# A two-layer decoder trunk on one core: weight products in runs of 16 hi parts and 16 lo parts

## The chip, the core and the metric

The kernel runs on one core of a Trainium2 chip. The metric is the device time of one execution in microseconds, the median of three runs. The engines that matter are TensorE (PE in the profile, with its weight loads shown apart as PEld), VectorE (DVE), ScalarE (ACT) and the queue of SyncE (SP), which issues the transfers of the weights.

## The reference

Two layers work on 256 tokens of 2048 features in float32. Each layer is a token mixer, a SwiGLU feed-forward block of 5632 hidden features and a gated per-layer embedding, each with an RMS norm ahead of it, and a final norm ends the trunk. The mixer of layer 0 is a Mamba-2 state-space mixer (an input projection to 10,304 columns, a convolution, a chunked scan, an output projection from 4096), that of layer 1 an RG-LRU (an input projection to 4096 columns, a convolution, block-diagonal gates, a scan, an output projection). Nearly all arithmetic is products of activations with weight matrices:

```python
h = h + mixer(rms_norm(h, norm_mix[i]))
v = rms_norm(h, norm_ffn[i])
gate, up = jnp.split(v @ w_ffn_in[i], 2, axis=-1)
h = h + (jax.nn.silu(gate) * up) @ w_ffn_out[i]
h = h + jax.nn.sigmoid(rms_norm(h, norm_ple[i]) @ w_ple_gate[i]) * (p[i] @ w_ple_up[i])
```

(The last lines are put in short form; the reference does the same in its own functions.)

## The kernel before

Activations lie with features on the 128 partitions and tokens on the free axis. A float32 operand of a product is held as two float32r parts, hi and lo, that add up to it. An activation operand x is one tile of 128 x 512: its hi part in the first 256 columns, its lo part in the last. A product of one weight block of 128 x 128 with one operand is two matmuls (`mm`, line 238): the weight's hi part times all 512 columns, which fills one bank of 512 columns, and the weight's lo part times the first 256, which is added to the bank's second half. They are called the hi product and the lo product here, and both together a pair. When all contraction tiles are done, `total` (line 147) adds the two halves of the bank: a copy on ScalarE (line 151) and an addition on VectorE (line 154).

Weights come as loads of 512 KB, as a rule two contraction tiles of 512 columns. `weights` (line 222) issues the transfer into one of five raw buffers, casts it to hi on ScalarE (line 234), subtracts to get lo on VectorE (line 235), with four hi tiles and four lo tiles of 1024 columns in rotation, and hands out both parts for two contraction tiles at a time.

`panel` (line 243) computes 512 output columns, as four blocks in four banks of the eight. For each contraction tile it runs four pairs, block by block, and then one step of other work (`shadow`): one of the queue `post`, which must follow the previous panel, and some of the queue `side`. The last two pairs of contraction tiles (`held=2`) are kept back and run block by block, so that the four banks finish one after another; in the very last panel of the kernel three are (`held=3`, line 676). `panel` is called by `ssd_mixer`, `lru_mixer`, `out_product`, `ffn`, `ple_up` and `ple`. The gates of the RG-LRU (line 548) call `mm` themselves.

The lines of the program are not the order of execution. The instructions of each engine are put in order when the kernel is built, by priority and by when their operands are expected, so two lines written hi, lo can stand apart on TensorE. Each engine then works strictly in its own order, and waits by semaphores for the others. At the end of the kernel, the last panel's four blocks go through sigmoid, product, addition to the residual (line 309), square and scaling, then come the last norm's root and the output.

Of the kernel before, what the change touches and what calls it, by code (L numbers as in the profile page):

```python
# [17 lines left out]
P = 128  # L18
T = 256                 # tokens
D = 2048  # L20
KT = D // P             # feature tiles of the residual
FFN = 5632
EPS = 1e-6
PW = 512                # output columns of one panel
NB = PW // P            # output tiles of one panel
KG = 2                  # contraction tiles of one weight load

# columns of the packed per-channel vectors
# [13 lines left out]
class Trunk:  # L42
    """Activations lie feature-major (feature on the partition, token on the free axis).

    A float32 operand of a product is held as two float32r parts, hi + lo, that add up to it
    exactly; a product is hi*hi + hi*lo + lo*hi in float32 accumulation.  An activation operand is
    one [128, 512] tile (hi | lo), so that the stationary weight's hi part streams both at once.
    """

    def __init__(self, ctx, tc):  # L50
        self.tc, self.nc = tc, tc.nc
        nc = self.nc
        pool = lambda name, bufs, **kw: ctx.enter_context(tc.tile_pool(name=name, bufs=bufs, **kw))
        self.const = pool("const", 1)
        self.act = pool("act", 48)
        self.wraw = pool("wraw", 5)
        self.wsp = pool("wsp", 4)
        self.tmp = pool("tmp", 2)
        self.ssd = pool("ssd", 2)
        self.ps = pool("ps", 8, space=bass.MemoryType.PSUM)  # L60
        self.side = deque()     # work in the shadow of the products, in small steps
        self.credit = 0.0
        self.last_table = None
        self.post = deque()     # what must follow a panel within the next one, in small steps

        c = self.const
        self.ident = c.tile([P, P], F32, name="ident")
        make_identity(nc, self.ident)
        self.identr = c.tile([P, P], F32R, name="identr")
        nc.vector.tensor_copy(self.identr, self.ident)  # L70
        self.sel = c.tile([P, 64], F32R, name="sel")
        nc.vector.tensor_tensor(self.sel, self.ident[:, :64], self.ident[:, 64:], ALU.add)
        self.ones = c.tile([P, P], F32, name="ones")
        nc.vector.memset(self.ones, 1.0)
        warm = c.tile([P, 1], F32, name="warm")
        nc.scalar.activation(warm, self.ones[:, :1], AF.Identity)
        # over (s, l) of one chunk, twice: s > l is put at -1e30
        mask = self.act.tile([P, 256], F32, name="mask", tag="a")
        nc.gpsimd.memset(mask, 0.0)
        for o in (0, P):  # L80
            nc.gpsimd.affine_select(
                out=mask[:, o:o + P], in_=mask[:, o:o + P],
                compare_op=ALU.is_ge, fill=-1e30, base=0, pattern=[[1, P]], channel_multiplier=-1)
        self.mask = c.tile([P, 256], F32R, name="maskr")
        nc.vector.tensor_copy(self.mask, mask)
        self.vecs = c.tile([P, NVEC], F32, name="vecs")
        self.h = c.tile([P, KT, T], F32, name="h")

# [6 lines left out]
    def table(self, out, in_, func, **kw):  # L95
        """An activation that needs its table: these keep program order, so that tables change seldom."""
# [34 lines left out]
    def split(self, src):  # L131
        """(hi | lo) operand of a [128, 256] float32 tile."""
        nc = self.nc
        x = self.act.tile([P, 2 * T], F32R, name="x", tag="a")
        nc.scalar.copy(x[:, :T], src)  # L135
        nc.vector.tensor_tensor(x[:, T:], src, x[:, :T].bitcast(F32), ALU.subtract)  # L136
        return x

    def split_scaled(self, src, w):
        """(hi | lo) operand of src * w, w one value per partition."""  # L140
# [6 lines left out]
    def total(self, b, t=None):  # L147
        """Sum of the two halves of a finished bank, in SBUF."""
# [24 lines left out]
    def rstd(self, acc, n, out, wait=4, last=False):  # L173
        """Appends to out 1 / sqrt(sum over partitions and tiles of acc / n + eps) per token, on
        every partition; in steps."""
# [12 lines left out]
        # a first guess, then Newton steps: on VectorE alone, or from the root's table where time is short  # L188
# [32 lines left out]

    def weights(self, w, width=PW, kt=KG, also=None):
        """Load w [128, kt, width]; gives its (hi, lo) parts for a few contraction tiles at a time."""
# [14 lines left out]
    def mm(self, b, hi, lo, x, first, last):  # L238
        nc = self.nc
        nc.tensor.matmul(b, hi, x, start=first, stop=False, skip_group_check=True)  # L240
        nc.tensor.matmul(b[:, T:], lo, x[:, :T], start=False, stop=last, skip_group_check=True)  # L241

    def panel(self, w, xs, pump=1.4, kt=KG, nb=NB, pre=None, post=True, held=2):
        """w [kg, 128, kt, nb*128] times the operands xs; returns the banks of the nb tiles.

        The last `held` weight tiles run block by block, so that the banks finish one after another.
        """
        banks = [self.bank() for _ in range(nb)]
        nk = w.shape[0] * kt
        k = 0  # L250
        rest = []

        def step(j, k, part):
            hi, lo = part
            self.mm(banks[j], hi[:, j * P:(j + 1) * P], lo[:, j * P:(j + 1) * P], xs[k], k == 0, k == nk - 1)

        def shadow():
            if post:
                self.advance(self.post)
            self.pump(pump)  # L260

        for g in range(w.shape[0]):
            for parts in self.weights(w[g], nb * P, kt, pre and (lambda: pre(g))):
                if k + len(rest) + held * len(parts) >= nk:
                    rest.extend(parts)
                    continue
                for i, part in enumerate(parts):
                    for j in range(nb):
                        step(j, k + i, part)
                    shadow()  # L270
                k += len(parts)
        for j in range(nb):
            for i, part in enumerate(rest):
                step(j, k + i, part)
            for _ in range((j + 1) * len(rest) // nb - j * len(rest) // nb):
                shadow()
# [5 lines left out]

    def norm_block(self, i, norm, layer, square=True):
        """Start the norm of residual block i: its square sum and its operand (without rstd)."""
# [16 lines left out]
    def norm_end(self, last=False):  # L301
        """The rstd of the norm, in steps: self.r."""
# [8 lines left out]
    def out_product(self, w, xs, norm, layer, pump=1.25, between=None, panels=range(D // PW)):  # L311
        """h += w^T xs; each finished block goes into the next norm (if there is one)."""
# [9 lines left out]

    def conv(self, t, cw, cb, ntap, i, out):
        """Causal depthwise convolution of t [128, 256] with its bias."""
# [6 lines left out]
    def softplus(self, v, n):  # L331
        """max(v, 0) + log1p(exp(-|v|)), the logarithm from its atanh series."""
# [17 lines left out]
    def ssd_mixer(self, w_dt, w_in, w_out, load):  # L350
# [3 lines left out]
        bc = [self.act.tile([P, 2, T], F32, name=f"bc{i}", tag="a") for i in range(8)]  # B, then C  # L354
# [20 lines left out]
        def dt_part(t):  # L375
# [11 lines left out]
            # columns: sums over chunk 0 | sums over chunk 1 | the latter from the start of chunk 0  # L387
# [4 lines left out]
            # the heads' hi parts on the lower partitions, their lo parts on the upper ones  # L392
# [15 lines left out]
        def of0(t):  # L408
            """The columns of a (s, l) tile whose s is in chunk 0."""
            return t[:, :384].rearrange("p (a b) -> p a b", a=3)[:, 0:3:2, :]  # L410

        def group(g, ts):
# [5 lines left out]
            # C B^T over (s, l) of the chunk pairs (0,0) (1,1) (0,1)  # L418
# [76 lines left out]
        # panels: C, dt (its 64 heads twice, on both halves of the partitions), B, x, z  # L495
# [18 lines left out]
    def lru_mixer(self, w_in, w_gates, w_out):  # L514
# [21 lines left out]
        def gates(q):  # L536
            """Blocks 2q and 2q+1 of the recurrence: channels 512 q .. 512 q + 511."""
# [3 lines left out]
            for m, (bias, dst) in enumerate((("lru_ba", rt), ("lru_bx", it))):  # L541
                ws = [t for ts in self.weights(w_gates[q, m], T, 4) for t in ts]
                for blk in range(2):
                    for j in range(2):
                        b = self.bank()
                        for k in range(2):
                            hi, lo = ws[blk * 2 + k]
                            self.mm(b, hi[:, j * P:(j + 1) * P], lo[:, j * P:(j + 1) * P],
                                    xop[q * 4 + blk * 2 + k], k == 0, k == 1)
# [21 lines left out]
            for j in range(4):  # L571
                self.table(th[j], th[j], AF.Sqrt, scale=2.0 ** 60)     # its table is poor near 0
# [50 lines left out]
    def ffn(self, layer, w_in, w_out, between):  # L623
# [18 lines left out]
        for g0, g1 in ((0, 6), (6, 11)):        # hidden panels that one pass of w_out takes  # L642
# [15 lines left out]
    def ple(self, w_gate, up, norm, nlayer):  # L658
# [15 lines left out]
        for n in range(D // PW):  # L674
            last = norm == "norm_final" and n == D // PW - 1
            ts = self.totals(self.panel(w_gate[n], u, held=3 if last else 2))
# [5 lines left out]
def trunk(ctx, tc, xT, pT, vecs, w_dt, w_ssd_in, w_ssd_out, w_lru_in, w_lru_gates, w_lru_out,  # L682
# [4 lines left out]
    def load(g):  # L687
        """The residual's blocks 2 g and 2 g + 1 and their operands."""
# [40 lines left out]

def _tiles(w, kg=KG, pw=PW):  # L730
    """[K, N] to [N / pw, K / (128 kg), 128, kg, pw]."""
# [4 lines left out]
def _cols(v):  # L736
    """[..., 128 n] to [128, ... n]."""
# [3 lines left out]
def _layout(a):  # L741
# [21 lines left out]
    g = np.stack([a["lru_wa"][0], a["lru_wx"][0]])              # [2, 8, 256, 256]  # L763
# [26 lines left out]
```

## Time and profile before

| | us |
|---|---|
| Median of three runs (lowest, highest) | 2738.17 (2736.03, 2739.68) |
| The profiled execution: span from first to last instruction | 2736.6 |
| TensorE products busy | 2707.5 |
| TensorE weight loads busy | 2339.8 |
| VectorE busy | 1887.4 |
| ScalarE busy | 1503.1 |
| Transfers | 495.24 MB, 181 GB/s in the mean |

The page gives no time of the profiled execution but its span, so the span is compared with the runs. A product's recorded duration reaches from its start to its modelled end, and neighbours overlap: 399 ns of a hi product's record stand beside a shorter distance between starts. Busy shares of TensorE are therefore read only to see that it hardly pauses. The first product starts 7.2 us into the span.

### The profile page before, as it was taken

The numbers are of one execution on the slowest core, as the hardware profiler recorded it, in microseconds if no ns is written. First come the engines' busy times: TensorE is split into PE (matmuls) and PEld (weight loads), VectorE is DVE, ScalarE is ACT, GpSimd is POOL, SyncE is SP. The second block draws the span as 40 slices with busy tenths as digits, with TensorE's granted clock in tenths as the row PEclk, the third lists the DMA queues.
The fourth block names the chain that finished last, engine by engine and source line by source line (L and its number), as shares of the span: only waits on it lengthen the run. The fifth ranks groups of instructions, "written<-read, shape, count | busy, mean of one in ns | idle before, by whom it ended". The sixth has DMA issues, their size and how long they took to land.

```text
span 2736.6 us, 40656 instructions
## 1 busy us (share of the span) xinstructions
PE 2707.5 (99%) x15488; PEld 2339.8 (85%) x15488; DVE 1887.4 (69%) x3130; ACT 1503.1 (55%) x2397; POOL 1.4 (0%) x9
## 2 busy tenths in 40 slices
PE   8999999999999999999999999999999999999997
PEld 7888888888888888888888888888888888888886
DVE  8887878856566655566666889987666555665666
ACT  7666665544454444444455678866444444444555
POOL 0000000000000000000000000000000000000000
PEclk9999999999999999999999999999999999999999
DMA  6544455565666666656665555566666665666653
GB/s 236 184 149 140 136 155 177 178 190 179 192 183 187 185 190 186 185 185 186 191 188 181 182 170 185 171 204 191 188 186 185 187 189 179 186 187 196 189 180 122
DMA packets 136708, 495.24 MB, mean 181 GB/s; under 512 B 15296, under 2 KB 15424, under 8 KB 136512
## 3 DMA queue, kind: packets, MB, share of 16 engines
q1 hardware_dynamic: 136512, 492.65, 58.5%
q8 instruction: 121, 1.98, 0.3%
q14 instruction: 75, 0.61, 0.1%
HBM read 490.49 MB, written 2.10 MB: 180 GB/s over the span
## 4 chain that ended last, share of the span: by engine, by line
PE 95%; DVE 3%; ACT 1%; issue 0%; DMA 0%; SPq 0%; DVEq 0%; ACTq 0%
PE bank L240 61%; PE bank L241 31%; DVE lo L235 1%; PE bank L461 1%; PE bank L447 0%; PE bank L445 0%; DVE c L328 0%; DVE hs L579 0%; PE bank L463 0%; PE bank L211 0%; PE bank L431 0%; DVE c L567 0%; ACT L97 0%; DVE t L154 0%; DVE th L576 0%
## 5 line engine op out<-in xcount | busy, mean ns | idle before, releaser
L240 PE MATMUL bank<-x,hi 128*128 128x512 f32 x7440 | 2632.0, 399 | 8.8 <-DVE x L144 7.2
L241 PE MATMUL bank<-x,lo 128*128 128x256 f32 x7440 | 2079.4, 281 | 5.9 <-DVE lo L235 5.9
L240 PEld LDWEIGHTS bank<-x,hi 128*128 128x128 f32 x7440 | 1396.8, 188 | 350.8 <-DVE x L144 7.2
L235 DVE TENSOR_TENSOR lo<-raw,hi 128x1024 fp32r<-128x1024 f32 x930 | 1134.4, 1222 | 722.8 <-ACT hi L234 719.7
L234 ACT CAST hi<-raw 128x1024 fp32r<-128x1024 f32 x930 | 972.2, 1049 | 892.9 <-PE bank L240 874.0
L241 PEld LDWEIGHTS bank<-x,lo 128*128 128x128 f32 x7440 | 1403.2, 189 | 12.4 <-DVE lo L235 10.2
L151 ACT COPY s<-bank 128x256 f32<-128x256 f32 x497 | 180.9, 370 | 225.3 <-PE bank L241 224.6
L154 DVE TENSOR_TENSOR t<-bank,s 128x256 f32<-128x256 f32 x449 | 186.8, 420 | 61.4 <-ACT s L151 59.4
L161 DVE TENSOR_TENSOR t<-t,r 128x256 f32<-128x256 f32 x217 | 88.5, 419 | 1.7
L328 DVE SCALAR_TENSOR_TENSOR c<-t,vecs,c 128x255 f32<-128x255 f32 (+2 forms) x144 | 63.9, 477 | 3.4 <-ACT c L326 3.0
L309 DVE TENSOR_TENSOR h<-h,t 128x256 f32<-128x256 f32 x144 | 60.0, 421 | 2.3
L97 ACT ACTIVATE e<-bank,ncs 128x256 f32<-128x256 f32 (+1 forms) x128 | 45.6, 418 | 15.7 <-PE bank L447 9.9
L97 ACT ACT_TABLE_LOAD x41 | 52.6, 1283 | 0.9 <-DVE c L328 0.2
L143 ACT ACTIVATE x<-h,vecs 128x256 fp32r<-128x256 f32 x96 | 48.1, 509 | 7.9 <-DVE h L309 5.9
L144 DVE SCALAR_TENSOR_TENSOR x<-h,vecs,x 128x256 fp32r<-128x256 f32 x96 | 45.3, 480 | 0.3 <-ACT x L143 0.2
L452 DVE TENSOR_TENSOR e<-e,cm 128x384 f32<-128x384 f32 x64 | 35.2, 555 | 14.9 <-ACT e L97 14.2
L97 ACT ACTIVATE sg<-t 128x256 f32<-128x256 f32 x88 | 36.5, 420 | 15.9 <-DVE t L161 15.9
L135 ACT CAST x<-t 128x256 fp32r<-128x256 f32 x88 | 36.0, 409 | 16.8 <-DVE t L638 16.8
L170 ACT ACTIVATE q<-h 128x256 f32<-128x256 f32 x104 | 42.2, 408 | 4.2 <-DVE h L309 1.9
L171 DVE TENSOR_TENSOR acc<-acc,q 128x256 f32<-128x256 f32 x104 | 43.5, 418 | 0.6
L638 DVE TENSOR_TENSOR t<-t,sg 128x256 f32<-128x256 f32 x88 | 36.9, 420 | 0.7
L136 DVE TENSOR_TENSOR x<-t,x 128x256 fp32r<-128x256 f32 x88 | 36.6, 416 | 0.0
(120 smaller groups left out, 652.6 us busy)
## 6 DMA issues: line engine op xcount, KB each, us to landing
raw<-in_w_ffn_in_dram SPq DMA_DIRECT2D x352, 512.0 KB, 4.2
raw<-in_w_ffn_out_dram SPq DMA_DIRECT2D x176, 512.0 KB, 4.2
raw<-in_w_ssd_in_dram SPq DMA_DIRECT2D x160, 512.0 KB, 4.1
raw<-in_w_ssd_out_dram SPq DMA_DIRECT2D x64, 512.0 KB, 3.7
raw<-in_w_ple_gate_dram SPq DMA_DIRECT2D x64, 512.0 KB, 4.1
raw<-in_w_lru_in_dram SPq DMA_DIRECT2D x64, 512.0 KB, 4.1
raw<-in_w_lru_out_dram SPq DMA_DIRECT2D x32, 512.0 KB, 4.2
raw<-in_w_ple_up_dram SPq DMA_DIRECT2D x8, 512.0 KB, 4.4
```

The source lines that it names most:

```text
L97: i = self.nc.scalar.activation(out, in_, func, **kw).ins
L143: nc.scalar.activation(x[:, :T], src, AF.Copy, scale=w)
L144: nc.vector.scalar_tensor_tensor(x[:, T:], src, w, x[:, :T].bitcast(F32), ALU.mult, ALU.subtract)
L151: nc.scalar.copy(s, b[:, T:])
L154: nc.vector.tensor_tensor(t, b[:, :T], s, ALU.add)
L161: self.nc.vector.tensor_tensor(t, t, r, ALU.mult)
L234: nc.scalar.copy(hi, src)
L235: nc.vector.tensor_tensor(lo, src, hi.bitcast(F32), ALU.subtract)
L240: nc.tensor.matmul(b, hi, x, start=first, stop=False, skip_group_check=True)
L241: nc.tensor.matmul(b[:, T:], lo, x[:, :T], start=False, stop=last, skip_group_check=True)
L309: self.nc.vector.tensor_tensor(hb, hb, t, ALU.add)
L328: nc.vector.scalar_tensor_tensor(out[:, d:], t[:, :T - d], self.vec(cw, (3 - d) * ntap + i), out[:, d:], ALU.mult, ALU.add)
```

## The change

`mm` is gone and `panel` is rewritten. Contraction tiles are gathered until 16 products of one kind can be made (`RUN // nb`, four tiles in a panel of four blocks) or the panel's tiles end. Then the group runs: first 16 hi products, tile by tile and block by block, then 16 lo products. In a panel's last group the lo products are sorted by block. In the very last panel of the kernel (`apart`) the last group runs block by block, each with its four hi and four lo products. A step of other work is issued whenever the products so far, a hi counted as two units and a lo as one, pass another 3 x nb units. The gates' pairs are written out in place and keep their order. Comments and docstrings are taken out elsewhere, which changes nothing.

```diff
+RUN = 16
...
-    def mm(self, b, hi, lo, x, first, last):
-        nc = self.nc
-        nc.tensor.matmul(b, hi, x, start=first, stop=False, skip_group_check=True)
-        nc.tensor.matmul(b[:, T:], lo, x[:, :T], start=False, stop=last, skip_group_check=True)
...
-    def panel(self, w, xs, pump=1.4, kt=KG, nb=NB, pre=None, post=True, held=2):
+    def panel(self, w, xs, pump=1.4, kt=KG, nb=NB, pre=None, post=True, apart=False):
+        nc = self.nc
         banks = [self.bank() for _ in range(nb)]
         nk = w.shape[0] * kt
+        todo = []
+        size = RUN // nb
+        count = [0, 0]
+
+        def product(j, k, part, lo):
+            b, x, wt = banks[j], xs[k], part[lo][:, j * P:(j + 1) * P]
+            if lo:
+                nc.tensor.matmul(b[:, T:], wt, x[:, :T], start=False, stop=k == nk - 1, skip_group_check=True)
+            else:
+                nc.tensor.matmul(b, wt, x, start=k == 0, stop=False, skip_group_check=True)
+
+            count[0] += 1 if lo else 2
+            while count[0] >= 3 * nb * (count[1] + 1):
+                count[1] += 1
+                if post:
+                    self.advance(self.post)
+                self.pump(pump)
+
+        def group(last):
+            if last and apart:
+                for j in range(nb):
+                    for lo in (0, 1):
+                        for k, part in todo:
+                            product(j, k, part, lo)
+            else:
+                for k, part in todo:
+                    for j in range(nb):
+                        product(j, k, part, 0)
+                order = [(j, k, part) for k, part in todo for j in range(nb)]
+                if last:
+                    order.sort(key=lambda o: o[0])
+                for j, k, part in order:
+                    product(j, k, part, 1)
+            todo.clear()
+
         k = 0
...
         for g in range(w.shape[0]):
             for parts in self.weights(w[g], nb * P, kt, pre and (lambda: pre(g))):
...
+                for part in parts:
+                    todo.append((k, part))
+                    k += 1
+                    if len(todo) == size or k == nk:
+                        group(k == nk)
...
-            ts = self.totals(self.panel(w_gate[n], u, held=3 if last else 2))
+            ts = self.totals(self.panel(w_gate[n], u, apart=last))
```

## Rows read from the trace of the kernel before

**Rows 1.** The page: the span, and busy us, share and instructions of each engine.

```profile
span 2736.6 us, 40656 instructions
PE 2707.5 (99%) x15488; PEld 2339.8 (85%) x15488; DVE 1887.4 (69%) x3130; ACT 1503.1 (55%) x2397; POOL 1.4 (0%) x9
```

**Rows 2.** The page's groups by line: busy us, mean ns | idle before, releaser.

```profile
L240 PE MATMUL bank<-x,hi 128*128 128x512 f32 x7440 | 2632.0, 399 | 8.8 <-DVE x L144 7.2
...
L235 DVE TENSOR_TENSOR lo<-raw,hi 128x1024 fp32r<-128x1024 f32 x930 | 1134.4, 1222 | 722.8 <-ACT hi L234 719.7
L234 ACT CAST hi<-raw 128x1024 fp32r<-128x1024 f32 x930 | 972.2, 1049 | 892.9 <-PE bank L240 874.0
```

**Rows 3.** Windows, hi products alone: length, PE busy (count), PEld, granted clock, DMA.

```profile
1000.00:1380.00 380.00, 380.00 (x1076) 202.06 (x1076) 1.00 0.62 188
...
1785.00:1890.00 105.00, 105.00 (x304) 56.81 (x303) 1.00 0.62 195
```

**Rows 4.** Timeline of TensorE, two stretches in alternation: start us, duration us, what.

```profile
20.29 0.39 PE L240 MATMUL bank<-x,hi 128*128 128x512 f32 x1
...
21.33 0.40 PE L240 MATMUL bank<-x,hi 128*128 128x512 f32 x1
...
900.22 0.40 PE L240 MATMUL bank<-x,hi 128*128 128x512 f32 x1
...
901.28 0.40 PE L240 MATMUL bank<-x,hi 128*128 128x512 f32 x1
```

**Rows 5.** Timeline of TensorE where products of one kind follow each other.

```profile
71.33 1.08 PE L240 MATMUL bank<-x,hi 128*128 128x512 f32 x4
...
1623.52 1.30 PE L240 MATMUL bank<-x,hi 128*128 128x512 f32 x5
1624.65 0.28 PE L241 MATMUL bank<-x,lo 128*128 128x256 f32 x1
...
1630.61 1.09 PE L240 MATMUL bank<-x,hi 128*128 128x512 f32 x4
1631.54 0.64 PE L241 MATMUL bank<-x,lo 128*128 128x256 f32 x4
1632.01 0.39 PE L240 MATMUL bank<-x,hi 128*128 128x512 f32 x1
...
1637.91 0.87 PE L240 MATMUL bank<-x,hi 128*128 128x512 f32 x3
1638.62 0.52 PE L241 MATMUL bank<-x,lo 128*128 128x256 f32 x3
...
1686.42 1.30 PE L240 MATMUL bank<-x,hi 128*128 128x512 f32 x5
1687.56 0.64 PE L241 MATMUL bank<-x,lo 128*128 128x256 f32 x4
1688.03 0.40 PE L240 MATMUL bank<-x,hi 128*128 128x512 f32 x1
...
1746.83 0.75 PE L241 MATMUL bank<-x,lo 128*128 128x256 f32 x5
1747.42 0.40 PE L240 MATMUL bank<-x,hi 128*128 128x512 f32 x1
...
2572.30 0.76 PE L240 MATMUL bank<-x,hi 128*128 128x512 f32 x2
```

**Rows 6.** Waits: who waited for whom, us in total, times, longest us.

```profile
ACT s L151 <- PE bank L241: 224.6, 297, 4.0
...
PE bank L241 <- DVE lo L235: 5.9, 7, 1.4
```

**Rows 7.** Timeline of the end: first copy, last lo product, last block's addition.

```profile
2713.49 0.37 ACT L151 COPY s<-bank 128x256 f32<-128x256 f32 x1 [4.02 <-PE bank L241]
...
2719.53 0.28 PE L241 MATMUL bank<-x,lo 128*128 128x256 f32 x1
...
2722.37 0.42 DVE L309 TENSOR_TENSOR h<-h,t 128x256 f32<-128x256 f32 x1
```

More of the change, by code (lines that the diff above doesn't have):

```diff
@@ L249, in panel @@
         nk = w.shape[0] * kt
-        k = 0
[L251 to L260, printed above, removed]
+        todo = []
[13 more added lines that the diff above has]
+                self.pump(pump)
@@ L262, in panel @@
+        k = 0
         for g in range(w.shape[0]):
             for parts in self.weights(w[g], nb * P, kt, pre and (lambda: pre(g))):
[L264 to L276, printed above, removed]
+                for part in parts:
[3 more added lines that the diff above has]
+                        group(k == nk)
@@ L547, in gates @@
                             hi, lo = ws[blk * 2 + k]
-                            self.mm(b, hi[:, j * P:(j + 1) * P], lo[:, j * P:(j + 1) * P],
-                                    xop[q * 4 + blk * 2 + k], k == 0, k == 1)
+                            x = xop[q * 4 + blk * 2 + k]
+                            nc.tensor.matmul(b, hi[:, j * P:(j + 1) * P], x,
+                                             start=k == 0, stop=False, skip_group_check=True)
+                            nc.tensor.matmul(b[:, T:], lo[:, j * P:(j + 1) * P], x[:, :T],
+                                             start=False, stop=k == 1, skip_group_check=True)
                         t = self.total(b)
```

## The prediction

> **What bounds the kernel now.** I read the page's busy shares first, then the groups by line, the waits, and last the order of the products in the timeline. TensorE is busy 2707.5 of 2736.6 us [rows 1], and VectorE and ScalarE, which convert the weights, are far from that (1134.4 and 972.2 us for their two conversion groups) [rows 2]. There are 7440 hi products and as many lo products. ScalarE waits 874.0 us in all for TensorE to give back a hi buffer [rows 2], while TensorE waits 5.9 us in all for a lo part [rows 6]. So supply runs ahead of use nearly everywhere, and the time is the number of pairs times the pace of a pair.
>
> A busy TensorE tells little, since the recorded 0.40 us of a hi product overlaps its neighbours. What counts is the distance from one start to the next. In the timeline three pairs take 1.06 us (900.22 to 901.28): 353.3 ns a pair. In a few stretches it is 1.04 us (20.29 to 21.33), 346.7 ns [rows 4]. The windows say the same: 380 us hold 1076 hi products, 353.2 ns each; the fast stretch has 304 in 105 us, 345.4 ns [rows 3]. Over all 7230 places where hi, lo, hi follow each other ([rows 4] are from two of their stretches) the mean is 235.7 ns from hi to lo and 116.7 from lo to hi: 352.4 ns. At the full granted clock of 1.00 [rows 3], and with no wait in it, this is the pace of the order itself. The two paces are two settled patterns for the same work, 6.7 ns apart.
>
> **What runs of one kind cost.** The change replaces hi, lo, hi, lo by 16 hi and then 16 lo. The trace of before already holds such runs, though short: where a lo part was late, the order on TensorE has two to five hi products in a row (29 places, 71.33 to 2572.30 us) and then the lo products. A merged row gives the distance, from its start to the start of the next row. Hi: five in 1.13 us and five in 1.14 us, so 0.226 and 0.228 each; four in 0.93 us, 0.2325 each; three in 0.71 us, 0.237 each [rows 5]. The longer the run, the cheaper its members: the first is as dear as in alternation (mean 234.6 ns over the undisturbed ones), the second 232.2, the third 228.8, the fourth 226.5. Lo: four in 0.47 us, twice, and five in 0.59 us: 0.1175 to 0.118 each [rows 5], against 116.7 in alternation, so a lo pays about a nanosecond.
>
> **The sum of the main term.** Hi run of 16: the four-run's 0.93 us, which holds the dear beginning, and 12 more at 0.227 make 3.65 us. Lo run: 16 x 0.118 = 1.89 us. Together 5.54 us against 16 x 352.4 ns = 5.64 us: 0.098 us less per group. The loads number 930 (of two contraction tiles of 512 columns, or the same volume), eight pairs each. Eight of them belong to the gates, whose products are only written out in place and keep their order; 7376 pairs are left, 461 groups. 461 x 0.098 = 45 us less.
>
> The bounds: with every hi at the three-run's 0.237 and every lo at 0.12, a group takes 5.71 us, 33 us more in all. With every hi at 0.226 and every lo at 0.113, the fast end of lo pitches in alternation, it takes 5.42 us, 100 us less. I take the middle, since the five-runs are the nearest rows to a run of 16.
>
> **The other parts.**
>
> *Side steps.* A step is issued for each 3 x nb units, a hi counting two and a lo one, so a panel still issues one step per contraction tile and a group four, about 1.4 us apart. No instruction is added. Cost 0; the side work's own products break a run only in the two mixer stages.
>
> *Buffers.* There are four hi and four lo tiles, and a group holds two of each. Both hi tiles are free 3.65 us into their group and are wanted again two groups after their own start, 11.1 us in; the lo tiles are free after 5.54 us and wanted 14.7 us in. One conversion takes 1.05 us on ScalarE and 1.22 on VectorE [rows 2], two of each per 5.54 us. The cover is some 7 us, and I put this at 0. If it were gone, a late conversion would cost up to its own 1.2 us for a group.
>
> *Late lo parts.* Where VectorE is the slower one, TensorE waits for lo: 5.9 us in seven places [rows 6]. A lo now comes up to 3.65 us later than its hi, longer than any of these waits, but VectorE is as loaded as before and may be late at the next one. I take 4 us less, bounds 0 and 6.
>
> *Panel ends.* Before, banks finish four pairs apart, 1.41 us; now the last group's lo products are sorted by block and finish four lo apart, 0.47 us. A bank costs a ScalarE copy of 0.37 us and a VectorE addition of some 0.42 [rows 7], so the four evacuations still keep up, but they end about 1 us after the last product, where three of them had ended before it. Four other banks are free for the next panel unless side work holds some, which happens in the 16 or so panels of the state-space mixer. ScalarE waits 224.6 us at these copies for TensorE [rows 6], so it is early there, not late. I take 2 us more, bounds 0 and 30 (a quarter microsecond at every one of about 117 panels).
>
> *The last panel.* Before, six contraction tiles ran block by block, so the banks were 6 x 0.353 = 2.12 us apart; now four do, 4 x 0.345 = 1.38 us apart. After the first copy at 2713.49 VectorE works through the four blocks and ends 9.3 us later (2722.79), some 2.2 us a block and 0.4 for the copy, 3.3 us after the last product's start at 2719.53 [rows 7]. With the first bank 3 x 0.74 us later relative to the last product and VectorE no faster, the tail grows by 2.2 us. Bounds 0 and 3.
>
> *The start.* The first products wait for the first operand; the first eight hi need only the first load, the next eight the second, which came before it was needed. Cost 0, bounds -1 and 1.
>
> **The time.** -45 - 4 + 2 + 2 = -45 us on the profiled span of 2736.6: 2691.6. The median of the runs, 2738.2, stands 1.6 us above that span, so I forecast 2693 us.
>
> **The rivals.**
>
> *The order is not kept* (2720). The runs in rows 5 exist because the instruction order is made by readiness, not by the program's lines alone. If lo products are put forward again, so that runs of four remain, a group costs four times 1.40 us (four hi and four lo, 1630.61 to 1632.01) = 5.60 us, and 461 x 0.04 = 18 us are saved. For: the cases in rows 5. Against: they stand where an operand was late, and supply is early nearly everywhere. Chance 0.09.
>
> *Panel ends take it back* (2723). Each of some 117 panels waits 0.25 us for a bank or a conversion behind the bunched evacuations: 30 us returned. Against it: ScalarE's waits. Chance 0.09.
>
> *The dear distance holds in a hi run* (2756). Three-runs at 0.237 show that a run can keep the dearer distance; if all 16 hi do so, with lo at 0.118, a group costs 5.68 us, 0.04 more than now, so 18 us are added (the other parts add up to nothing). The place is every group; it turns from gain to loss where the mean hi distance passes 0.234 us, (5.64 - 1.89) / 16. For: 353.3 ns is by far the commoner pace now. Against: in both five-runs the distance fell to 0.227 after the first product and stayed. Chance 0.09.
>
> *The fall goes on* (2591). From 0.237 in three-runs to 0.2325 and 0.227; should the remaining eleven drop to 0.216 and lo to 0.113, a group takes 1.13 + 11 x 0.216 + 1.81 = 5.32 us, 0.32 less, and 147 us go. No distance after a hi in rows 4 or 5 supports 0.216; the fourth and fifth of the five-runs stand still at 226 to 227. Chance 0.05.
>
> The Trainium skill, "TensorE: Matmul & The Clock Gate", section "Back-to-back issue gap", puts the distance of back-to-back products at full clock at columns / 2.4 + 2.5 ns; as an estimate that is 215.8 and 109.2 ns, and some 200 us saved. By that rule neither alternation nor runs should cost what they do here; the trace has 0.226 and 0.1175 in its best runs [rows 5], so I keep the rows.
>
> **How the numbers follow.** Forecast 0.68, with a range of its own of 2675 to 2712 (bounds of the side terms, and a hi distance of 0.2245 to 0.2295 us). The rivals have 0.09, 0.09, 0.09 and 0.05. The range of 2668 to 2728 takes in the first two rivals and leaves out the dear distance, the further fall and the edges. A change of 0.2%, 5.5 us, is about what a measurement tells from none. Faster: the forecast, the fall, and most of the first two rivals, 0.86; slower: most of the dear-distance rival and a piece of the panel ends, 0.08; same 0.06.
>
> **What would show it.** In the profile after, merged rows of 16 hi followed by 16 lo, 3.65 and 1.89 us from start to start; hi products in a pure stretch 346 ns of window per product; no new wait of TensorE at panel starts; four copies at a panel's end about 0.47 us apart; the last bank's chain ending some 5.5 us after the last product's start. The forecast is wrong if a hi run takes more than 3.75 us, if runs are cut short away from side work, or if the first product of a panel waits for a bank.

## The result, and the profile after

The kernel after takes 2706.26 us (2705.53 to 2707.99, four runs), the kernel before beside it 2738.41 us (2736.03 to 2739.68): a ratio of 0.9884 (95% interval 0.987 to 0.9898), 32 us less. The forecast was 2693 us, 45 us less.

The page of after: the span, busy us of the engines, and the groups by line (busy us, mean ns | idle before, releaser). They answer to [rows 1, 2].

```profile
span 2704.2 us, 40787 instructions
...
PE 2676.0 (99%) x15488; PEld 2349.6 (87%) x15488; DVE 1828.5 (68%) x3130; ACT 1501.4 (56%) x2397; POOL 1.4 (0%) x9
...
L258 PE MATMUL bank<-x,hi 128*128 128x512 f32 x7376 | 1781.0, 392 | 8.6 <-DVE x L145 7.9
...
L256 PE MATMUL bank<-x,lo 128*128 128x256 f32 x7376 | 972.0, 283 | 1.2 <-DVE lo L236 1.0
```

TensorE has the same 15488 products and is as full as before; so the span has to be read by distances between starts again. The timeline of after in the stretch of [rows 4] and in the fast stretch of before:

```profile
902.43 3.82 PE L258 MATMUL bank<-x,hi 128*128 128x512 f32 x16
906.08 2.08 PE L256 MATMUL bank<-x,lo 128*128 128x256 f32 x16
907.99 3.82 PE L258 MATMUL bank<-x,hi 128*128 128x512 f32 x16
...
1787.63 3.82 PE L258 MATMUL bank<-x,hi 128*128 128x512 f32 x16
1791.28 2.08 PE L256 MATMUL bank<-x,lo 128*128 128x256 f32 x16
1793.19 3.82 PE L258 MATMUL bank<-x,hi 128*128 128x512 f32 x16
```

The order is kept: 16 hi, 16 lo, 16 hi. A hi run takes 3.65 us (902.43 to 906.08), a lo run 1.91 (906.08 to 907.99), a group 5.56. Taken over all undisturbed groups (those that no wait and no product of the side work breaks, some 380 of the 461), the distance from one start to the next in a hi run is, by position, 233.4, 235.8, 228.3, 232.5, 230.8 and then eleven times 226.7 ns: 3654.5 ns. In a lo run it is 113.3, 119.2 and then fourteen times 120.0: 1912.5 ns. Together 5567 ns, 347.9 a pair, where alternation took 352.4. At 1790 us nothing is gained: there the fast pattern of alternation already took 346.7 ns a pair, which is 226.7 + 120.

The window of [rows 3] over the hi products of after (length, PE busy and count, PEld, granted clock, DMA): 380 / 1092 = 348.0 ns each, at the same granted clock.

```profile
1000.00:1380.00 380.00, 260.59 (x1092) 200.25 (x1090) 1.00 0.57 187
```

The waits of all engines (us in total, times, longest), of which ScalarE's two answer to [rows 2, 6]:

```profile
ACT hi L235 <- PE bank L258: 966.3, 624, 3.1
...
ACT s L152 <- PE bank L256: 9.7, 11, 3.5
```

And those of TensorE alone:

```profile
PE bank L415 <- DVE sp L362: 2.9, 1, 2.9
...
PE bank L256 <- DVE lo L236: 1.0, 2, 0.6
PE bank L566 <- DVE lo L236: 0.9, 2, 0.7
...
PE bank L258 <- DVE up L155: 0.7, 2, 0.4
```

TensorE waits 1.0 us for lo parts where it waited 5.9 [rows 6], and ScalarE still waits (966.3 us) for hi buffers to come free, so supply is early as before. The bunched banks show at the copies of the finished banks: ScalarE waited 224.6 us before them [rows 6] and now 9.7. New is one wait of 2.9 us where the state-space mixer transposes its step sizes, and two short ones at the panels of `w_ple_up`. The tail of after:

```profile
2682.32 0.37 ACT L152 COPY s<-bank 128x256 f32<-128x256 f32 x1 [3.50 <-PE bank L256]
...
2685.86 0.64 PE L256 MATMUL bank<-x,lo 128*128 128x256 f32 x4
...
2689.91 0.42 DVE L324 TENSOR_TENSOR h<-h,t 128x256 f32<-128x256 f32 x1
```

The last of these four lo starts at 2686.22, and the last block's addition ends at 2690.33, 4.1 us after it, where it took 3.3 [rows 7].

### The profile page after: what moved, and what is told of

Same layout as the page of the kernel before. It is cut to its first block, busy times and chain, and to the rows that moved or that the text cites. A ratio compares the mean times of both kernels' runs of the same rounds, so it can differ in the third digit from the quotient of the medians.

```text
span 2704.2 us, 40787 instructions
## 1 busy us (share of the span) xinstructions
PE 2676.0 (99%) x15488; PEld 2349.6 (87%) x15488; DVE 1828.5 (68%) x3130; ACT 1501.4 (56%) x2397; POOL 1.4 (0%) x9
## 3 DMA queue, kind: packets, MB, share of 16 engines
q8 instruction: 121, 1.98, 0.3%
## 4 chain that ended last, share of the span: by engine, by line
PE 95%; DVE 3%; ACT 1%; issue 0%; DMA 0%; SPq 0%; DVEq 0%; ACTq 0%
PE bank L258 60%; PE bank L256 31%; DVE lo L236 1%; PE bank L476 1%; PE bank L564 1%; PE bank L462 0%; PE bank L446 0%; PE bank L460 0%; ACT hi L235 0%; PE bank L478 0%; PE bank L212 0%; DVE t L155 0%; PE bank L566 0%; DVE xc L343 0%; DMA raw<-in_w_ssd_in_dram 0%
## 5 line engine op out<-in xcount | busy, mean ns | idle before, releaser
L258 PE MATMUL bank<-x,hi 128*128 128x512 f32 x7376 | 1781.0, 392 | 8.6 <-DVE x L145 7.9
L258 PEld LDWEIGHTS bank<-x,hi 128*128 128x128 f32 x7376 | 1352.8, 188 | 271.8 <-DVE x L145 8.5
L235 ACT CAST hi<-raw 128x1024 fp32r<-128x1024 f32 x930 | 973.5, 1050 | 1023.4 <-PE bank L258 966.3
L236 DVE TENSOR_TENSOR lo<-raw,hi 128x1024 fp32r<-128x1024 f32 x930 | 1103.4, 1218 | 483.3 <-issue 430.7
L256 PEld LDWEIGHTS bank<-x,lo 128*128 128x128 f32 x7376 | 951.8, 191 | 40.8 <-DVE lo L236 1.9
L256 PE MATMUL bank<-x,lo 128*128 128x256 f32 x7376 | 972.0, 283 | 1.2 <-DVE lo L236 1.0
L155 DVE TENSOR_TENSOR t<-bank,s 128x256 f32<-128x256 f32 x449 | 162.9, 416 | 284.4 <-ACT s L152 283.9
L152 ACT COPY s<-bank 128x256 f32<-128x256 f32 x497 | 161.7, 374 | 21.7 <-PE bank L256 9.7
L324 DVE TENSOR_TENSOR h<-h,t 128x256 f32<-128x256 f32 x144 | 53.7, 416 | 0.0
L482 DVE SCALAR_TENSOR_TENSOR y<-xs,vecs,bank 128x256 f32<-128x256 f32 x32 | 15.3, 479 | 31.9 <-PE bank L478 31.9
L341 ACT ACTIVATE c<-t,vecs 128x256 f32<-128x256 f32 x48 | 27.0, 594 | 12.1 <-DVE t L162 12.1
```

The costliest lines, as they stand in the source:

```text
L152: nc.scalar.copy(s, b[:, T:])
L155: nc.vector.tensor_tensor(t, b[:, :T], s, ALU.add)
L235: nc.scalar.copy(hi, src)
L236: nc.vector.tensor_tensor(lo, src, hi.bitcast(F32), ALU.subtract)
L256: nc.tensor.matmul(b[:, T:], wt, x[:, :T], start=False, stop=k == nk - 1, skip_group_check=True)
L258: nc.tensor.matmul(b, wt, x, start=k == 0, stop=False, skip_group_check=True)
```

## The experiments

Three theories of why the pair got cheaper were set against each other. A: each kind of product has a settled distance, and a change from one kind to the other costs. B: a lo that adds into the bank its hi has just written costs. C: the gain is late lo parts no longer waited for. "Waits" of a kernel below is one sum from its trace: by how much the distances between starts go beyond what is usual at that place in a run; it is 24.3 us for after. It also holds what a lower clock costs. In the profiled runs with groups of 4, groups of 8, block by block and without sorting, the granted clock fell to 0.50 for 10.2 us in all between the start and the tail, and 4 to 5 us of each one's sum are products in these stretches; before and after have no such stretch.

**Groups of 4.**

```
-RUN = 16
+RUN = 4
```

> Groups of 4 hi and 4 lo instead of 16 (RUN = 4), all else as in the kernel after. Theory A (each kind of product has one settled distance in a run, 226.7 ns for hi and 120 for lo; what costs is the change from lo to hi, where the first five hi take 233, 236, 228, 232 and 231 ns, 27 ns over the settled ones, while the first lo give 7.5 ns back): a group of 4 takes 233.4 + 235.8 + 228.3 + 232.5 + 113.3 + 119.2 + 2 x 120 = 1402 ns, 350.6 a pair against 347.9 with 16, so 20 us more than the kernel after, about 2726 us. Theory B (alternation is dear because each lo product adds into the bank that its own hi product has just written; in a group the next product always goes to another bank): nothing changes with the size, 2706. Theory C (the gain is that TensorE no longer waits for late lo parts): some of the waits come back, 2708 to 2712, with the distances in runs unchanged.

2746.45 us, ratio to before 1.0028 (1.0018 to 1.0037). The timeline:

```profile
900.71 1.09 PE L258 MATMUL bank<-x,hi 128*128 128x512 f32 x4
901.64 0.64 PE L256 MATMUL bank<-x,lo 128*128 128x256 f32 x4
902.12 1.09 PE L258 MATMUL bank<-x,hi 128*128 128x512 f32 x4
```

A group takes 928.8 + 473.9 = 1402.7 ns, 350.7 a pair, as A has it. But the kernel got slower than before, 20 us above A's figure: its waits are 43.6 us, 19 more than in after. Among them are these two, at the panels of `w_ple_up` and in the tail, where the banks now finish close together:

```profile
PE bank L258 <- DVE up L155: 10.9, 4, 2.9
...
PE bank L183 <- DVE acc L172: 5.6, 1, 5.6
```

**Groups of 8** (`RUN = 8`).

> Groups of 8 and 8 (RUN = 8). Theory A: 1161 + 3 x 226.7 = 1841 ns for hi and 113.3 + 119.2 + 6 x 120 = 952 for lo, 349.2 a pair, 9 us more than the kernel after, about 2716 us. Theory B: 2706. Theory C: 2706 to 2709.

2731.31 us, ratio 0.997 (0.9958 to 0.9981). From the first hi to the next lo run 1.85 us in the timeline:

```profile
902.02 2.00 PE L258 MATMUL bank<-x,hi 128*128 128x512 f32 x8
903.87 0.40 PE L256 MATMUL bank<-x,lo 128*128 128x256 f32 x2
```

On average 1841.7 + 952.3 ns, 349.2 a pair, as A says; the waits are 42.7 us, again 18 more than in after, so the time stands 15 us above A's figure.

**Groups of 32** (`RUN = 32`).

> Groups of 32 and 32 (RUN = 32), two groups to a panel of 16 contraction tiles, four weight loads to a group, with the same four hi and four lo tiles. Theory A: 16 further pairs at 346.7 in each group, 347.3 a pair, 4 to 5 us less than the kernel after, about 2702 us, if the four lo tiles, all of one group, are still filled in time for the next; TensorE's waits for lo parts show whether they are. Theory B: 2706. Theory C: 2706 or more.

2736.42 us, ratio 0.9989 (0.998 to 0.9998): the pace improves and nearly all of the gain is lost.

```profile
903.52 7.44 PE L258 MATMUL bank<-x,hi 128*128 128x512 f32 x32
910.80 4.00 PE L256 MATMUL bank<-x,lo 128*128 128x256 f32 x32
914.63 0.63 PE L258 MATMUL bank<-x,hi 128*128 128x512 f32 x2
```

11.11 us for 32 pairs, 347.2 each. The waits are 55.9 us, spread over the mixers and the feed-forward blocks. A group now holds all four hi and all four lo tiles, so the next group's conversions can start only as this group's products release a tile. TensorE's waits for lo parts, 1.0 us in after, are one part of the loss:

```profile
PE bank L256 <- DVE lo L236: 4.9, 6, 2.1
```

**Groups of 32 with more tiles.** Six hi and six lo tiles; the pool of activations shrinks to make room.

```
-RUN = 16
+RUN = 32
-        self.act = pool("act", 48)
+        self.act = pool("act", 40)
-        self.wsp = pool("wsp", 4)
+        self.wsp = pool("wsp", 6)
```

> Groups of 32 with six hi and six lo tiles instead of four (and 40 instead of 48 activation tiles, to make room). With four tiles the distances in runs were 226.7 and 120 as in groups of 16, but some 30 us more were lost in waits. Theory A with the tiles as the cause of these waits: most of them go, 347.3 ns a pair and 2702 to 2712 us. If the raw buffers (five, unchanged) or the bunched side work are the cause, it stays above 2725.

2710.82 us, ratio 0.9903 (0.9888 to 0.9918). The waits fall from 55.9 to 31.6 us: most of what groups of 32 lost was the tiles. They are still 7 us above those of after.

**The lo product one pair later.** The kernel before, in alternation, but each lo follows the hi of the next block: it adds into a bank that was written a pair earlier.

```
+            self.nc.tensor.matmul(banks[j], hi[:, j * P:(j + 1) * P], xs[k], ...)
+            lo_product()              # the one kept by the step before
+            due.append((j, k, lo))
```

> The kernel before, with hi and lo still in alternation, but each lo product comes one pair later: hi of block j, then lo of block j-1, so that a lo no longer adds into the bank that the product just ahead has written (only in the last quarter of a panel, which runs block by block, is it the same bank). Theory A: kind changes at every product as before, so the pace stays 352 to 353 ns a pair and the time 2738 us (or, should it settle in the other pattern of 346.7 ns, that pattern in most stretches, near 2700; then the trace has 346.7 alone). Theory B: the bank clash is gone from three quarters of the pairs, their pace falls to 347 or less, near 2705 us, while the block by block quarter keeps 353.

2736.23 us, ratio 0.999 (0.9981 to 1.0).

```profile
900.07 0.40 PE L263 MATMUL bank<-x,hi 128*128 128x512 f32 x1
900.30 0.28 PE L258 MATMUL bank<-x,lo 128*128 128x256 f32 x1
...
901.13 0.40 PE L263 MATMUL bank<-x,hi 128*128 128x512 f32 x1
```

Three pairs in 1.06 us, as in [rows 4]; over 7004 places 235.2 + 116.8 = 352.0 ns. Both patterns are there, as in before. Another bank changes nothing, so B falls.

**Each kind block by block in every group.** Four hi in a row add into one bank, then four into the next.

```
-                for k, part in todo:
-                    for j in range(nb):
-                        product(j, k, part, 0)
...
+                order = [(j, k, part) for j in range(nb) for k, part in todo]
+                for lo in (0, 1):
+                    for j, k, part in order:
+                        product(j, k, part, lo)
```

> Groups of 16 as in the kernel after, but each kind runs block by block in every group: four products into one bank, then four into the next, so that each product adds into the bank and columns that the one just ahead has written. Theory A (the distance depends on the kind of product and on changes of kind alone): 226.7 and 120 ns in runs as in the kernel after, about 2706 us. Theory B (adding into the bank that has just been written is dear): three of four products become dearer, by some 7 ns each if the loss of the alternation is the measure, 16 x 0.75 x 2 x 7 = 168 ns a group and 77 us more, about 2783. That alternation with the lo put off by one pair was as slow as before speaks for A.

2718.63 us, ratio 0.9925 (0.9909 to 0.9942).

```profile
902.03 3.82 PE L258 MATMUL bank<-x,hi 128*128 128x512 f32 x16
905.69 2.08 PE L256 MATMUL bank<-x,lo 128*128 128x256 f32 x16
907.60 3.82 PE L258 MATMUL bank<-x,hi 128*128 128x512 f32 x16
```

The distances are those of after, position by position (233.4, 235.8, 228.4, 232.5, 230.9, 226.7; 113.6, 119.7, 120). B falls a second time. The 12 us come from waits (37.3 against 24.3 us), 7.6 of them at the panels of `w_ple_up`, which come in four pairs.

**No sorting of the last group.** After, but a panel's last lo products stay in the order of the others.

```
-                if last:
-                    order.sort(key=lambda o: o[0])
```

> The kernel after without the sorting in a panel's last group: its 16 lo products go tile by tile there too, so the four banks finish within four products, 0.12 us apart, instead of 0.48. It tells what the second half of the change is worth. If the sorting only spreads the evacuations, they now come in one bunch and end about 1 us later: nothing on TensorE where the next panel has other banks, and up to 1 us at each of the eight ple_up panels and the out products before them and at some mixer panels, 5 to 10 us more in all, 2711 to 2716 us. If panel ends are hidden altogether, 2706. Distances in runs unchanged in both.

2717.63 us, ratio 0.993 (0.9904 to 0.9956): the second half of the change is worth 11 us. The distances are unchanged; the waits are 36.3 us, and nearly all the excess stands at the panels of `w_ple_up`, which are only one load long:

```profile
1377.00 1.11 PE L256 MATMUL bank<-x,lo 128*128 128x256 f32 x8
1379.76 1.61 PE L258 MATMUL bank<-x,hi 128*128 128x512 f32 x6 [1.65 <-DVE up L155]
...
1415.38 5.50 PE L258 MATMUL bank<-x,hi 128*128 128x512 f32 x16 [1.98 <-ACT hi L235]
1420.72 0.52 PE L256 MATMUL bank<-x,lo 128*128 128x256 f32 x3
```

The second wait costs more than itself. Behind it 16 hi take 5.34 us (1415.38 to 1420.72) instead of 3.65, and the window over most of that stretch (length, PE busy and count, granted clock, DMA) shows why:

```profile
1416.00:1419.00 3.00, 3.00 (x9) 0.50 0.00 0
```

The granted clock was 0.50 there, the lower of its two levels (1.2 GHz), after TensorE had waited 1.65 us and, some 36 us later, 1.98 us. About 3 of the 11 us are such products at the panels of `w_ple_up`.

In after the same kind of place waits 0.36 us, and the clock doesn't fall:

```profile
1408.09 1.11 PE L256 MATMUL bank<-x,lo 128*128 128x256 f32 x8
1409.57 1.20 PE L258 MATMUL bank<-x,hi 128*128 128x512 f32 x4 [0.36 <-DVE up L155]
```

**A shorter lo.** After, with a lo product that streams 128 of its 256 columns.

```
-  nc.tensor.matmul(b[:, T:], wt, x[:, :T], ...)
+  nc.tensor.matmul(b[:, T:T + P], wt, x[:, :P], ...)
```

> The kernel after, with the lo product streaming only the first 128 of its 256 columns (half of the tokens' lo terms are left out). It measures what holds a lo run at 120 ns a product. If it is the columns plus a fixed part, as 226.7 = 512/2.4 + 13.3 and 120 = 256/2.4 + 13.3 suggest, lo falls to 66.7 ns and the kernel to some 2706 - 0.85 x 7376 x 0.0533 = 2370 us or more, with other engines in the way. If it is the weight load that goes with every product, lo stays near 113 to 120 ns and the time within 50 us of the kernel after.

2704.3 us in its one run: with half the columns in 7376 products it stands 2 us below after.

```profile
899.56 3.90 PE L258 MATMUL bank<-x,hi 128*128 128x512 f32 x16
903.30 1.90 PE L256 MATMUL bank<-x,lo 128*128 128x128 f32 x16
905.03 3.90 PE L258 MATMUL bank<-x,hi 128*128 128x512 f32 x16
```

A lo now takes 111.9 ns instead of 120, so at 128 columns something other than the columns sets the distance. The Trainium skill, "TensorE: Matmul & The Clock Gate", section "LDWEIGHTS (loading the stationary operand)", gives a weight load as its columns / 1.2, as an estimate 106.7 ns for 128. That is near 111.9, but this run's own records of weight loads last 189 ns (hi) and 192 ns (lo) in the mean, and no run separates the load from the product, so what sets the 111.9 stays open. The lo runs save 0.18 us a group, and the hi run gives 0.08 back, 3.74 us: its first distance is 292 ns, and ten products pass until 226.7 is reached. So the dear beginning of a run depends on what went before it. That leaves 0.094 us a group, 43 us in all, which the time does not show: the waits are some 35 us longer than in after, and about 15 us of them are products at a granted clock of 0.50, which this run has for 34 us between start and tail.

**Alternation with equal lengths, 512.** The kernel before with a lo that streams all 512 columns (it adds lo·lo).

```
-        nc.tensor.matmul(b[:, T:], lo, x[:, :T], start=False, ...)
+        nc.tensor.matmul(b, lo, x, start=False, ...)
```

> The kernel before, in alternation, with the lo product streaming all 512 columns into the whole bank, as the hi product does (it adds the product of the two lo parts, which the kernel leaves out). Kinds still alternate in weights, lengths don't. If the loss in alternation comes from the change of length, every product takes 226.7 ns, 453.3 a pair, and the kernel 2736 + 7440 x 0.1009 = 3487 us. If it comes from changing weight parts or tiles or from any other part of the alternation, a pair keeps a loss of 6.7 ns or more, 460 and above, and the time is 3537 us or more.

3483.89 us.

```profile
900.16 0.39 PE L241 MATMUL bank<-x,lo 128*128 128x512 f32 x1
...
901.98 0.39 PE L241 MATMUL bank<-x,lo 128*128 128x512 f32 x1
```

Eight products in 1.82 us; over 7315 places each 226.7 and 227.0 ns, the settled distance of a long run. Changing kind and weights at every product costs nothing here.

**Alternation with 512 and 384.** The same line with `b[:, P:]` and `x[:, :3 * P]`.

> The kernel before, in alternation, with the lo product streaming 384 columns (x from column 0 to 383, into columns 128 to 511 of the bank, so that the sums are not the reference's). In alternation with 512 and 512 columns there was no loss. If any change of length costs, a pair takes 226.7 + 173.3 and 6 to 7 ns, 406 to 407 ns, and the kernel 2736 + 7440 x 0.054 = 3138 us. If only a product that is hardly longer than its weight load (112 ns at least, by the run with 128 columns) brings the loss, a pair takes 400 ns and the kernel about 3090 us.

3179.74 us, above both figures expected.

```profile
900.23 0.40 PE L240 MATMUL bank<-x,hi 128*128 128x512 f32 x1
...
902.30 0.40 PE L240 MATMUL bank<-x,hi 128*128 128x512 f32 x1
```

Five pairs in 2.07 us; on average 237.2 + 175.9 = 413.1 ns. A line through 226.7 at 512 and 120 at 256 columns gives 173.3 for 384, so a pair without loss would take 400 ns. By that line, which no run of 384-column products alone has checked, the loss is 13.1 ns, about twice that of 512 with 256. Without the line at least 6.6 ns are shown: 553 of 560 undisturbed blocks of twelve pairs take 413.3 ns a pair, and five take 406.7. It is not the shortness of the lo that costs: a longer one cost no less.

**Alternation with equal lengths, 256.** The kernel before with a hi of 256 columns, into the other half of the bank.

```
-        nc.tensor.matmul(b, hi, x, start=first, ...)
+        nc.tensor.matmul(b[:, :T], hi, x[:, :T], start=first, ...)
```

> The kernel before, in alternation, with the hi product streaming 256 columns too, into the bank's first half (the hi part's product with the lo part of the activations is left out). All products are short and of one length. If a change of length is what costs, the distance is 120 ns from each product to the next, as in a lo run; if short products as such bring a loss outside of runs of one kind, it is 123 ns or more. The whole time says little, since the conversions of the weights take 1.05 and 1.22 us for every 8 pairs and may become the bound: the distances in undisturbed stretches decide.

2092.38 us.

```profile
900.08 0.28 PE L240 MATMUL bank<-x,hi 128*128 128x256 f32 x1
...
901.03 0.28 PE L240 MATMUL bank<-x,hi 128*128 128x256 f32 x1
```

Eight products in 0.95 us, 120 ns each at over 13,000 undisturbed places (elsewhere TensorE now waits for the conversions). With short products of equal length there is no loss either. Theory A stands, made narrower: a loss was seen only where the length changes. It isn't there at every change, though. In the fast pattern of before [rows 4] the lengths alternate too, and its 346.7 ns are 226.7 + 120 with nothing lost; of 536 undisturbed blocks of twelve pairs 65 run in it, the others at 353.3.

**Groups of 32 where supply allows.** Six tiles of each kind, groups of 16 in the mixers and of 32 in the feed-forward and `ple` panels.

```
+        self.run = RUN
-        size = RUN // nb
+        size = self.run // nb
...
+        k.run = RUN          # before the mixers of a layer
+        k.run = 2 * RUN      # before its feed-forward part
```

> A candidate: six hi and six lo tiles (40 activation tiles), groups of 16 in the two mixers and of 32 in the feed-forward and embedding stages, where groups of 32 had no waits once there were six tiles. 592 of 930 loads lie there, so by theory A 0.64 x 7376 x 0.6 ns = 3 us are saved on the kernel after, and the tail is some 1.5 us shorter, as in the run with 32 and six tiles: about 2702 us. If fewer activation tiles hold up the mixers, 2706 or more.

2704.11 us (2702.56 to 2704.9), ratio 0.9885 (0.9866 to 0.9904), waits 23.7 us. After has 0.9884: the two can't be told apart, and no version tried beats after by more than is measured.

## Why the prediction was right, and where its size was off

*The mechanism.* The pace of a pair is what moved. By distances between starts, the hi products lost 58.2 us over the whole span (1769.5 to 1711.3) and the lo products gained 25.9 (876.9 to 902.8). Those sums hold the waits too; the undisturbed groups alone make 461 x 0.0717 = 33.1 us, and the other terms nearly cancel.

*The hi run* was forecast at 3.65 us and took 3654.5 ns. That the distance settles near 0.227 was read rightly from the five-runs [rows 5]. The size of the dear beginning was in part luck. The five-runs had one dear product, which would have given 1.13 + 11 x 0.227 = 3.63 us; the sum took the four-run's 0.93 instead, which is what the first four of a long run cost. "The longer the run, the cheaper its members" did not hold product by product: the mean of 226.5 for the fourth was that of the two five-runs alone, and in after the fourth takes 232.5, the fifth 230.8, and 226.7 begins with the sixth.

*The lo run is the term that was mis-sized*: "Lo run: 16 x 0.118 = 1.89 us". It took 1912.5 ns. A run of four or five begins with a cheap lo of 113, so its mean of 0.1175 to 0.118 hides the 120 of the later ones; the settled member had to be read, as was done for hi, not the mean of a short run. 0.0245 us by 461 groups is 11 of the missing 13 us.

*What the pair's loss is.* The prediction had a dear beginning but no cause. The runs show where the loss stands: alternation loses 6.7 ns a pair in its common pattern, 5.7 on average, with lengths 512 and 256, 13.1 with 512 and 384 (by the line above), and none with 512 and 512 or 256 and 256; the bank plays no part. In groups, one change there and back costs 16 ns in groups of 4 and 20 in groups of 8, 16 and 32. So groups of 16 pay 20 ns in 16 pairs where alternation paid 91, and 461 x 0.071 is the 33 us. Why a change of length costs, and whether 384 really costs more than 256, stays open; so does what picks between the two patterns of alternation [rows 4], of which one loses nothing.

*Late lo parts*: 4 us forecast. Waits over 0.3 us for lo fell from 7.0 to 2.5 us. Theory C is right for this much and no more.

*Panel ends, new waits*: 2 us forecast. The panels of `w_ple_up` cost 1 us and the step sizes of the state-space mixer 2.9, which no step had named. One of the prediction's own signs of being wrong did come: the first product of a panel waited for a bank, at two places and 0.7 us in all, too little to matter. The four copies of a panel's end ran back to back, as this row of after's timeline (start us, us, count) shows, so they started behind the banks rather than 0.47 us apart with them; TensorE did not wait for them elsewhere.

```profile
583.49 1.33 ACT L152 COPY s<-bank 128x256 f32<-128x256 f32 x4
```

The run without sorting shows that this small price is owed to the sorting: 11 us more without it.

*The tail* grew by 0.9 us against 2.2: from the start of the last lo to the end of the span 17.94 us after 17.09. VectorE's chain of the last block ended 4.1 us after the last product's start, not 5.5. *The start* cost 1 us, the upper bound. Side steps cost nothing that the runs show; the tiles were enough for 16, and the two runs with 32 show the price of that cover when it is gone: 24 us of waits, the difference that six tiles made.

The sum: -33.1 - 4.5 + 2.9 + 1 + 1 + 0.9 = -31.8 us, and the span fell by 32.4.

*The rivals.* The order was kept. Panel ends took back 4 us, not 30. The dear distance held for five products, not sixteen. The fall stopped at 226.7 and 120. The Trainium skill, "TensorE: Matmul & The Clock Gate", section "Back-to-back issue gap", gives columns / 2.4 + 2.5 ns as the gap of a single product taken by itself (215.8 and 109.2 as estimates), and for a stream of weight loads and products about 131 ns at 512 columns and 81 at 128. No run here met either: the settled distances, each with its own weight load, lie 13.3 ns above columns / 2.4 at 512 and 256 columns, and at 128 the distance was 111.9.

## What to carry to other kernels

Where TensorE is full, read the distance from one start to the next, per position in a run, and take the settled member of a run, not the mean of a short one. Put matmuls of equal length next to each other, in groups that leave operand tiles free, so that the conversions stay ahead: groups that held half of the tiles did so here, groups that held all of them did not. Let the banks of a group finish one after another where a short panel wants them back at once: the pace was worth 33 us here, and the wrong end of a panel or too few tiles would have taken back 11 and 30. Look at the granted clock behind such a wait, since a wait of 2 us was followed by products at 0.50.

## What was not expected of the hardware

A 512-column product with its weight load takes 226.7 ns, a 256-column one 120.0, and a 128-column one still 111.9: half the columns gained 8 ns. Alternating lengths cost 6.7 ns a pair in the common pattern (512 and 256), and 13.1 with 512 and 384 by a line between the other lengths, with nothing waiting and at a granted clock of 1.00 [rows 3]. After 256-column products it takes five of 512 columns until the distance settles, after 128-column ones ten. At a place where TensorE had waited 1.98 us behind two short panels, the granted clock fell to 0.50 and 16 hi took 5.34 us instead of 3.65.
